# First mixer: the rows of a block inversion in sixteen pieces between the heads' queries and values

## The chip, the core and the metric

One core of one Trainium2 chip runs the whole program. The metric is the time of one execution on the device in microseconds. The engines named below are PE (TensorE: matmuls and transposes through the identity), DVE (VectorE), ACT (ScalarE), POOL (GpSimd) and SP (SyncE, which here only issues DMAs).

## What is computed

The program is a decoder trunk of two layers on 512 tokens of width 1024, in float32. Each layer is a SwiGLU block, a mixer, and another SwiGLU block. The change touches the mixer of the first layer, which runs two groups of heads on one normalised input and projects their concatenation:

```python
def even_mixer(u, w_in, conv_w, a_log, dt_bias, head_norm_w, w_out):
    '''Parallel head groups: dilated sliding-window attention (A) | gated DeltaNet (B).'''
    proj = (u @ w_in).astype(jnp.float32)
    ...
    o_a = dilated_window_attention(qa, ka, va)          # 8 heads of 64
    qkv_b = jax.nn.silu(causal_dwconv(qkv_b, conv_w))   # 4 heads of 128
    ...
    o_b = gated_delta_rule(l2norm(qb), l2norm(kb), vb, g, beta)
    o_b = rmsnorm(o_b, head_norm_w) * jax.nn.silu(z.reshape(bsz, seq, B_HEADS, B_HEAD_DIM))
    o = jnp.concatenate([o_a..., o_b...], axis=-1)
    return (o @ w_out).astype(u.dtype)

def gated_delta_rule(q, k, v, g, beta):
    ...
    a_mat = jnp.where(strict, jnp.einsum('bnhid,bnhjd->bnhij', k_beta, kc) * decay, 0.0)
    t_mat = a_mat + jnp.eye(B_CHUNK, dtype=a_mat.dtype)
    u = lax.linalg.triangular_solve(t_mat, vc * bc, left_side=True, lower=True, unit_diagonal=True)
    w = lax.linalg.triangular_solve(t_mat, k_beta * jnp.exp(gc)[..., None], ...)
    ...
    def step(state, inp): ...      # over the chunks, one after the other
```

The kernel works with 4 chunks of 128 tokens. The triangular systems are solved by an explicit inverse: the 32x32 blocks on the diagonal are inverted row by row on DVE, and two doubling steps with matmuls make 128x128 inverses of them.

## The kernel before

**The mixer.** `even_mixer` has two streams of work. `gated_delta` computes the DeltaNet heads in this order: `keys(h)` for four heads, `invert32` (the 32x32 inverses, for all heads and chunks at once), `queries(h)`, `values(h)`, the two doubling steps (lines 766 to 777), the products with the inverse (780 to 785) and the recurrence over four chunks (787 to 814). I call the part from line 765 to 814 the solve. `attention` computes the attention heads two by two: projections of q and k (each 24 matmuls of 512 columns), projections of the values va for four heads at a time, and for each head four blocks of scores with their softmax (PE, DVE, ACT, DVE, ACT, PE).

**The order.** Both are Python generators. `attention` yields, after each piece that it has written, a number that stands for the piece's length: 5.2 for q or k, 2.6 for each of four pieces of va, and 0.3, 0.6, 0.9 and 1.2 for the four softmax blocks of a head. `gated_delta` yields how much of the attention is to be written next, and the loop (`need -= next(fill, need)`) writes pieces until that is used up; what a piece goes over is lost. What remains of the attention is written when `gated_delta` has ended. After it come the gates (line 900 on), with four projections Z of 24 matmuls each, and the mixer's output product.

The order of writing is a priority: the framework that compiles the kernel orders each engine's instructions ahead of time, by priority, and where the next one isn't ready in its own plan, it puts a later one in its place. On the chip each engine then runs its list in that fixed order. Tiles of one name take turns in a fixed number of slots: `scr` (`scratch()`, 128x512) has 2, `feat` has 2, the PSUM banks `mm` have 2 and `acc` 4. A tile that is written into a slot waits for the last reader of the one that was there.

**The inversion.** `invert32` stops at two yields. Up to the first it stores A to DRAM and loads it in another layout (`nb`, line 707, in a slot of `U`); the result tile `tb` takes one of the two slots of `feat`. Behind it: one ACT instruction turns the sign (711), and a loop of 31 rows follows. Row i is a product (718) of `n x m` elements on DVE into the scratch tile `pr` and a sum over m of it (719) into row i of `tb`, from which the next row reads. `pr` is taken once (line 710), ahead of the loop, and is held to its end. Then one DMA writes `tb` to DRAM (720) and eight DMAs bring the pieces to their places in `Tm` (723).

**Scratch elsewhere.** `queries(h)` takes three scratch tiles: `th` in `conv_silu` (478 and 479), `sq` (737, read by 740) and `er` (a DMA by SP, line 557, then exp on ACT, 746, and a product on POOL, 747). `values(h)` takes one (`th`) and one slot of `feat`; `Rk` (782, POOL) takes one for each head in the solve.

Of the kernel before, what the change touches and what calls it, by code (L numbers as in the profile page):

```python
# [30 lines left out]
class Trunk:  # L31
# [540 lines left out]
    def even_mixer(self, w_in, conv_w, a_log, dt_bias, head_norm_w, w_out, post_w, next_pre):  # L572
# [8 lines left out]
        with ExitStack() as ctx:  # L581
# [52 lines left out]
            def t4(name, bufs=HB):  # L634
                return gp.tile([128, TT, 128], F32, name=name, bufs=bufs)

            def two(name):
                return gp.tile([128, 2 * TT, 128], F32, name=name, bufs=2)

            def transposed(x):  # L640
                p = blocks(self.ps("acc"))
                for c in range(TT):
                    nc.tensor.transpose(p[:, c, :], x[:, c, :], self.ident)
                return p

            def four(lhs, rhs):
                p = blocks(self.ps("acc"))
                for c in range(TT):
                    nc.tensor.matmul(p[:, c, :], lhs[:, c, :], rhs[:, c, :], start=True, stop=True)  # L649
                return p  # L650

            def feature(j, p, out=None):

                out = t4("feat", 2) if out is None else out
                self.conv_silu(p, taps(j), None, out.rearrange("p c t -> p (c t)"))
                return out

            def project(j):
                p = self.ps("mm")
                self.product(p, self.w_cols(w_in, CONV0 + j * 128))  # L660
                return p
# [31 lines left out]
            def invert32():  # L693


                nb = two("U").rearrange("p a b -> p (a b)").rearrange("p (j i) -> p j i", i=32)
                tb = t4("feat", 2).rearrange("p c t -> p (c t)").rearrange("p (i c) -> p i c", c=16)
                ablk = self.dram.tile([4, HB * TT, 32, 32], F32, name="ablk")
                tblk = self.dram.tile([2, 4, HB * TT, 32, 16], F32, name="tblk")
                for b in range(4):  # L700
                    s = slice(32 * b, 32 * b + 32)
                    nc.sync.dma_start(ablk[b].rearrange("q j i -> j q i"), AT[s, :, s])
                nc.gpsimd.memset(Tm, 0.0)
                nc.gpsimd.memset(tb, 0.0)
                for e in range(2):
                    half = slice(64 * e, 64 * e + 64)
                    nc.sync.dma_start(nb[half], ablk.rearrange("b q j i -> (b q) j i"))
                    nc.gpsimd.memset(tb[half, 16 * e:16 * e + 16, :].rearrange("p a b -> p (a b)")[:, ::17], 1.0)
                yield
                pr = self.scratch()  # L710
                nc.scalar.activation(nb, nb, AF.Copy, scale=-1.0)

                nc.gpsimd.memset(nb.rearrange("p a b -> p (a b)")[:, 16 * 33::33], 1.0)
                for i in range(1, 32):
                    n, m = min(i, 16), i + (i >= 16)
                    q = pr[:, :n * m].rearrange("p (c m) -> p c m", c=n)
                    a = nb[:, :m, i:i + 1].rearrange("p m o -> p o m").to_broadcast([128, n, m])
                    tt(q, a, tb[:, :m, :n].rearrange("p m c -> p c m"), op=OP.mult)
                    nc.vector.tensor_reduce(tb[:, i, :n], q, axis=mybir.AxisListType.X, op=OP.add)
                nc.sync.dma_start(tblk.rearrange("e b q i c -> (e b q) i c"), tb)  # L720
                for e in range(2):
                    for b in range(4):
                        nc.sync.dma_start(Tm[32 * b:32 * b + 32, :, 32 * b + 16 * e:32 * b + 16 * e + 16],
                                          tblk[e, b].rearrange("q i c -> i q c"))
                yield

            def values(h):
                vt = t4("vt")
                tt(vt, transposed(feature(2 * HB + h, project(2 * HB + h))), over(col(kl, h)), op=OP.mult)
                return vt  # L730
# [19 lines left out]
            def gated_delta():  # L750
                heads = range(HB)
                K = []
                for h in heads:
                    K.append(keys(h, first[h]))
                    yield 4
                inv = invert32()
                next(inv)
                Q = []
                for h in heads:
                    Q.append(queries(h, *K[h][1:]))  # L760
                    yield 4
                next(inv)
                vt = [values(h) for h in heads]
                yield 4
                U = [part(x, i) for x in (two("U"), two("U")) for i in range(2)]
                for h in heads:
                    nc.scalar.copy(U[h], transposed(part(Tm, h)))
                for l in range(2):
                    for h in heads:
                        Al = t4("kT")  # L770
                        nc.gpsimd.tensor_tensor(Al, part(AT, h), lmask[:, l:l + 1, :].to_broadcast([128, TT, 128]),
                                                op=OP.mult)
                        X = t4("kT")
                        nc.scalar.copy(X, four(Al, part(Tm, h)))
                        tt(U[h], U[h], four(X, U[h]), op=OP.subtract)
                        if l == 0:
                            nc.scalar.copy(part(Tm, h), transposed(U[h]))
                wT = [part(AT, h) for h in heads]
                for h in heads:
                    k = K[h][0]  # L780
                    Rk = blocks(self.scratch())
                    nc.gpsimd.tensor_tensor(Rk, k, over(col(egc, h)), op=OP.mult)
                    nc.scalar.copy(wT[h], four(Rk, U[h]))
                    tt(vt[h], four(U[h], vt[h]), over(col(beta, h)), op=OP.mult)
                    nc.gpsimd.tensor_tensor(k, k, over(col(edec, h)), op=OP.mult)
                S = None
                for c in range(TT):
                    vn = [vt[h][:, c, :] for h in heads]
                    if c:
                        p = blocks(self.ps("acc"))  # L790
                        for h in heads:
                            nc.tensor.matmul(p[:, h, :], wT[h][:, c, :], S[:, h, :], start=True, stop=True)
                        for h in heads:
                            stt(vn[h], p[:, h, :], nbeta[:, c, h:h + 1], vn[h], op0=OP.mult, op1=OP.add)
                    if c + 1 < TT:
                        p = blocks(self.ps("acc"))
                        for h in heads:
                            nc.tensor.matmul(p[:, h, :], K[h][0][:, c, :], vn[h], start=True, stop=True)
                        Sn = t4("S", 2)
                        if S is None:  # L800
                            nc.scalar.copy(Sn, p)
                        else:
                            for h in heads:
                                stt(Sn[:, h, :], S[:, h, :], egl[:, c, h:h + 1], p[:, h, :], op0=OP.mult, op1=OP.add)
                    o = blocks(self.ps("acc"))
                    for h in heads:
                        if c:
                            nc.tensor.matmul(o[:, h, :], Q[h][:, c, :], S[:, h, :], start=True, stop=False)
                        nc.tensor.matmul(o[:, h, :], K[h][2][:, c, :], vn[h], start=c == 0, stop=True)
                    S = Sn  # L810
                    nc.scalar.copy(ob[:, c, :, :], o)
                    junk = self.scratch()
                    for h in heads:
                        nc.scalar.activation(junk[:, :128], ob[:, c, h, :], AF.Square, accum_out=os_[:, c, h:h + 1])

                flat = lambda x: x.rearrange("p c h -> p (c h)")
                rq = self.rstd(flat(qs), 1, 128.0 ** -0.5)
                for _ in range(2):
                    tt(flat(os_), flat(os_), rq, op=OP.mult)
                r = self.rstd(flat(os_), 128)  # L820
                tt(flat(os_), r, rq, op=OP.mult)
# [79 lines left out]
            for need in gated_delta():  # L901
                while need > 0:
                    need -= next(fill, need)
# [322 lines left out]
```

## Time and profile before

| | us |
|---|---|
| three runs, median | 2157.63 |
| three runs, lowest and highest | 2151.29 and 2346.45 |
| the profiled execution | 2155.2 |
| its span, first to last instruction | 2153.4 |

The page gives busy times and shares of the span for each engine, the chain of work that ended last, and the costliest groups of instructions. Answers of the trace give the same for a stretch of the span, in us from its start. A matmul's record overlaps that of the next one, so PE counts as busy as long as matmuls follow each other closely; what is missing from a full stretch is time in which PE stood. The mixer of the first layer lies between about 365 and 690 us, and the inversion's rows between 493 and 559 us.

### The profile page before, as it was taken

Reading aid. Unit: us, or ns where it says so; the run is one execution under the profiler, and the core shown is the slowest. Engines: PE = TensorE matmul, PEld = TensorE weight load, DVE = VectorE, ACT = ScalarE, POOL = GpSimd, SP = SyncE. Lnnn points to the kernel's source line nnn. Section 1 sums busy time; section 2 is a strip of 40 time slices with the busy share of each in tenths; the row PEclk is TensorE's granted clock in tenths of the full one; section 3 lists DMA queues with packets and bytes.
Section 4 is the critical chain, followed back from the end, with each engine's and each line's share of the span. In section 5 each row is a group of like instructions: output and inputs, shape, how many; then the busy total and the mean of one; then the engine's idle time right before and its main releaser. Section 6 shows DMA issues by size and latency. Waiting matters only on the chain.

```text
span 2153.4 us, 33155 instructions
## 1 busy us (share of the span) xinstructions
PE 2111.5 (98%) x13311; PEld 1871.1 (87%) x13311; DVE 1477.5 (69%) x2329; ACT 1024.9 (48%) x1577; POOL 149.5 (7%) x142
## 2 busy tenths in 40 slices
PE   8999999999999999999999999999999999999998
PEld 7999988887788999988899998887777788999986
DVE  5867656869667676656677765678887846867663
ACT  4444553455564444444344454347565423544541
POOL 0011000111110011000001100000000000011000
PEclk9999999999999999999999999999999999999999
DMA  8587424442423588443557842333433236587421
GB/s 235 138 195 159 135 90 138 108 117 56 108 69 98 149 205 185 118 137 108 146 127 181 186 130 93 98 96 90 116 101 100 84 118 157 138 198 160 122 89 68
DMA packets 284037, 277.06 MB, mean 129 GB/s; under 512 B 18576, under 2 KB 244552, under 8 KB 283884
## 3 DMA queue, kind: packets, MB, share of 16 engines
q1 hardware_dynamic: 243308, 228.81, 35.4%
q0 software_dynamic: 40576, 46.14, 12.9%
q8 instruction: 104, 1.70, 0.3%
q14 instruction: 49, 0.40, 0.1%
HBM read 265.93 MB, written 4.79 MB: 126 GB/s over the span
## 4 chain that ended last, share of the span: by engine, by line
PE 84%; DVE 6%; DMA 4%; ACT 3%; issue 2%; POOL 0%; SPq 0%; DVEq 0%; POOLq 0%; ACTq 0%
PE mm L300 18%; PE acc L300 13%; PE acc L235 9%; PE acc L236 9%; PE acc L237 9%; PE mm L167 4%; PE mm L168 4%; PE mm L169 4%; DMA wraw<-in_ffn_w_up_dram 2%; DMA M<-rows_o 1%; PE acc L649 1%; PE acc L169 1%; PE acc L168 1%; PE acc L167 1%; DVE wlo L81 1%
## 5 line engine op out<-in xcount | busy, mean ns | idle before, releaser
L80 ACT CAST whi<-wraw 128x1024 fp32r<-128x1024 f32 x296 | 310.0, 1048 | 396.1 <-PE acc L237 107.4
L81 DVE TENSOR_TENSOR wlo<-wraw,whi 128x1024 fp32r<-128x1024 f32 x292 | 356.8, 1223 | 148.8 <-ACT whi L80 147.0
L80 ACT CAST whi<-wq 128x1024 fp32r<-128x1024 f32 x144 | 151.1, 1049 | 244.7 <-issue 77.6
L167 PE MATMUL mm<-uhi,whi 128*128 128x512 f32 (+1 forms) x712 | 264.5, 372 | 2.1 <-DVE feat L476 1.2
L168 PE MATMUL mm<-ulo,whi 128*128 128x512 f32 (+1 forms) x712 | 262.7, 369 | 0.3 <-DVE ulo L81 0.3
L169 PE MATMUL mm<-uhi,wlo 128*128 128x512 f32 (+1 forms) x712 | 262.6, 369 | 0.0
L81 DVE TENSOR_TENSOR wlo<-wq,whi 128x1024 fp32r<-128x1024 f32 x144 | 175.6, 1222 | 97.3 <-ACT whi L80 93.1
L235 PE MATMUL acc<-whi,hs 128*128 128x512 f32 x576 | 227.2, 395 | 0.0
L236 PE MATMUL acc<-wlo,hs 128*128 128x512 f32 x576 | 227.2, 394 | 0.0
L300 PE MATMUL mm<-uhi,whi 128*128 128x256 f32 x576 | 164.4, 285 | 4.4 <-DVE q L388 4.4
L380 POOL DMA_DIRECT2D wq<-in_ffn_w_up_dram x72 | 92.7, 1291 | 1073.9 <-DMA wq<-in_ffn_w_gate_dram 243.3
L300 PE MATMUL mm<-uhi,wlo 128*128 128x256 f32 x576 | 163.7, 284 | 0.0
L300 PE MATMUL mm<-ulo,whi 128*128 128x256 f32 x576 | 163.6, 284 | 0.0
L300 PE MATMUL acc<-uhi,whi 128*128 128x256 f32 x576 | 162.8, 283 | 0.0
L300 PE MATMUL acc<-uhi,wlo 128*128 128x256 f32 x576 | 162.8, 283 | 0.0
L300 PE MATMUL acc<-ulo,whi 128*128 128x256 f32 x576 | 162.8, 283 | 0.0
L167 PEld LDWEIGHTS mm<-uhi,whi 128*128 128x128 f32 x712 | 134.3, 189 | 27.8 <-issue 4.2
L168 PEld LDWEIGHTS mm<-ulo,whi 128*128 128x128 f32 x712 | 134.7, 189 | 23.6 <-issue 4.1
L169 PEld LDWEIGHTS mm<-uhi,wlo 128*128 128x128 f32 x712 | 134.7, 189 | 22.8 <-issue 3.4
L237 PE MATMUL acc<-whi,hs 128*128 128x512 f32 x384 | 151.5, 395 | 0.0
L236 PEld LDWEIGHTS acc<-wlo,hs 128*128 128x128 f32 x576 | 108.4, 188 | 25.2
L235 PEld LDWEIGHTS acc<-whi,hs 128*128 128x128 f32 x576 | 108.5, 188 | 25.2
(393 smaller groups left out, 5280.0 us busy)
## 6 DMA issues: line engine op xcount, KB each, us to landing
wraw<-in_ffn_w_down_dram SPq DMA_DIRECT2D x88, 512.0 KB, 3.5
wq<-in_ffn_w_gate_dram SPq DMA_DIRECT2D x72, 512.0 KB, 5.6
wq<-in_ffn_w_up_dram POOLq DMA_DIRECT2D x72, 512.0 KB, 8.0
wraw<-in_ffn_w_gate_dram SPq DMA_DIRECT2D x52, 512.0 KB, 5.6
wraw<-in_ffn_w_up_dram SPq DMA_DIRECT2D x52, 512.0 KB, 6.4
wraw<-in_odd_w_in_dram SPq DMA_DIRECT2D x40, 512.0 KB, 4.0
wq<-in_ffn_w_up_dram SPq DMA_DIRECT2D x36, 512.0 KB, 3.8
wraw<-in_even_w_in_dram SPq DMA_DIRECT2D x28, 512.0 KB, 4.6
```

Of the source, the lines that this page charges most:

```text
L80: nc.scalar.copy(hi, src)
L81: (nc.gpsimd if on_pool else nc.vector).tensor_tensor(lo, src, hi.bitcast(F32), op=OP.subtract)
L167: nc.tensor.matmul(p, whi[:, k, :], hi, start=k == 0, stop=False)
L168: nc.tensor.matmul(p, whi[:, k, :], lo, start=False, stop=False)
L169: nc.tensor.matmul(p, wlo[:, k, :], hi, start=False, stop=k == KD - 1)
L235: nc.tensor.matmul(p, ahi, hi, start=k == 0, stop=False)
L236: nc.tensor.matmul(p, ahi, lo, start=False, stop=False)
L237: nc.tensor.matmul(p, alo, hi, start=False, stop=k == nk - 1)
L300: self.nc.tensor.matmul(p[:, f * 256:(f + 1) * 256].rearrange("p (t c) -> p t c", c=128), l, r, start=new and f == k == i == 0, stop=f == ...
L380: nc.gpsimd.dma_start(raw, src, accum_op=OP.add)
L649: nc.tensor.matmul(p[:, c, :], lhs[:, c, :], rhs[:, c, :], start=True, stop=True)
```

## The change

The rows are divided into sixteen pieces. `invert32` yields after a row when the rows so far have reached the next sixteenth of a sum in which row i counts 300 + 2·min(i,16)·i; the pieces are rows 1 to 5, 6 to 9, 10 to 12, 13 to 14, 15 to 16, 17 to 18, 19, 20 to 21, 22 to 23, 24, 25, 26 to 27, 28, 29, 30 and 31. The last one ends with the DMAs of lines 720 and 723. Three pieces are written after each head's queries and one after each head's values. `pr` is now taken anew for every row.

The attention's share is changed too: 5 instead of 4 after each head's keys, 1.7 after each of the three pieces behind a head's queries (4 before, once a head), and 2 after each head's values (4 before, once for all). By the lengths that `attention` yields, and with what pieces go over, 48.4 of it stood ahead of the solve before (q and k of the first two pairs, va and the softmax of heads 0 to 3, and q of the third pair), and 70.0 now: also k of the third pair, va of heads 4 to 7 and the softmax of heads 4 and 5. Behind it remain q and k of the last pair and the softmax of heads 6 and 7. Nothing is computed differently, and the number of instructions of each kind is the same.

```diff
                 yield
-                pr = self.scratch()
                 nc.scalar.activation(nb, nb, AF.Copy, scale=-1.0)
 
                 nc.gpsimd.memset(nb.rearrange("p a b -> p (a b)")[:, 16 * 33::33], 1.0)
+
+                steps, size = 0, lambda i: 300 + 2 * min(i, 16) * i
+                total = sum(size(i) for i in range(1, 32))
                 for i in range(1, 32):
+                    pr = self.scratch()
                     n, m = min(i, 16), i + (i >= 16)
                     q = pr[:, :n * m].rearrange("p (c m) -> p c m", c=n)
                     a = nb[:, :m, i:i + 1].rearrange("p m o -> p o m").to_broadcast([128, n, m])
                     tt(q, a, tb[:, :m, :n].rearrange("p m c -> p c m"), op=OP.mult)
                     nc.vector.tensor_reduce(tb[:, i, :n], q, axis=mybir.AxisListType.X, op=OP.add)
+                    if i < 31 and sum(size(r) for r in range(1, i + 1)) * 16 >= total * (steps + 1):
+                        steps += 1
+                        yield
...
                 for h in heads:
                     K.append(keys(h, first[h]))
-                    yield 4
+                    yield 5
                 inv = invert32()
                 next(inv)
                 Q = []
                 for h in heads:
                     Q.append(queries(h, *K[h][1:]))
-                    yield 4
-                next(inv)
-                vt = [values(h) for h in heads]
-                yield 4
+                    for _ in range(3):
+                        next(inv, None)
+                        yield 1.7
+                vt = []
+                for h in heads:
+                    vt.append(values(h))
+                    next(inv, None)
+                    yield 2
+                for _ in inv:
+                    pass
```

## Rows read from the trace of the kernel before

**Rows 1.** The page: span, and busy time, share and instructions of two engines.

```profile
span 2153.4 us, 33155 instructions
PE 2111.5 (98%) x13311; PEld 1871.1 (87%) x13311; DVE 1477.5 (69%) x2329; ACT 1024.9 (48%) x1577; POOL 149.5 (7%) x142
```

**Rows 2.** The page: chain of work that ended last, shares by engine.

```profile
PE 84%; DVE 6%; DMA 4%; ACT 3%; issue 2%; POOL 0%; SPq 0%; DVEq 0%; POOLq 0%; ACTq 0%
```

**Rows 3.** Windows (stretch, length, busy PE PEld DVE ACT POOL, PEclk, DMA share, GB/s).

```profile
444.00:493.00 49.00, 49.00 (x250) 39.07 (x249) 30.57 (x67) 29.65 (x63) 7.84 (x6) 1.00 0.45 115
493.00:559.00 66.00, 60.24 (x317) 48.17 (x317) 63.06 (x142) 29.58 (x57) 6.77 (x5) 0.97 0.27 75
559.00:626.00 67.00, 66.34 (x463) 57.68 (x464) 33.17 (x92) 41.63 (x108) 15.71 (x13) 1.00 0.24 61
```

**Rows 4.** Waits of PE from 493 to 560 us: total, times, longest.

```profile
PE tr L847 <- ACT P L840: 2.3, 1, 2.3
PE tr L847 <- DVE h L858: 2.0, 1, 2.0
PE mm L167 <- DVE feat L476: 1.2, 2, 0.7
```

**Rows 5.** Window, columns as in Rows 3, around and behind the wait of 2.0 us.

```profile
507.00:515.00 8.00, 6.19 (x21) 4.42 (x22) 6.79 (x23) 2.97 (x8) 0.17 (x1) 0.79 0.25 66
```

**Rows 6.** Groups on DVE, 493 to 559 us: busy us, mean ns, idle before.

```profile
L718 DVE TENSOR_TENSOR scr<-U,feat 128x1 f32<-128x1 f32 (+30 forms) x31 | 18.7, 603 | 0.2
L719 DVE TENSOR_REDUCE feat<-scr 128x1 f32<-128x1 f32 (+30 forms) x31 | 12.4, 400 | 0.2
```

**Rows 7.** Timeline of DVE: first row, the last values, the last row.

```profile
493.42 0.16 DVE L718 TENSOR_TENSOR scr<-U,feat 128x1 f32<-128x1 f32 x1
...
536.53 0.67 DVE L729 TENSOR_TENSOR vt<-acc,kl 128x512 f32<-128x512 f32 x1
...
557.83 0.69 DVE L719 TENSOR_REDUCE feat<-scr 128x16 f32<-128x512 f32 x1
```

**Rows 8.** Timeline of SP behind the last row: start us, us.

```profile
558.55 0.34 SPq L720 DMA_DIRECT2D tblk<-feat  x1
...
560.58 4.32 SPq L723 DMA_DIRECT2D h<-tblk  x8
```

**Rows 9.** Scratch slots on POOL: start us, us, idle before and its releaser.

```profile
455.92 1.29 POOL L747 TENSOR_TENSOR qf<-qf,scr 128x512 f32<-128x512 f32 x1 [1.24 <-ACT scr L746]
534.73 1.05 POOL L782 TENSOR_TENSOR scr<-k,egc 128x512 f32<-128x512 f32 x1 [27.56 <-DVE feat L479]
558.60 1.96 POOL L782 TENSOR_TENSOR scr<-k,egc 128x512 f32<-128x512 f32 x1 [21.09 <-DVE feat L719]
```

**Rows 10.** Timeline of SP and ACT: two scratch tiles `er` and the sign.

```profile
448.98 0.35 SPq L557 DMA_DIRECT2D scr<-rows_e  x1
457.03 1.06 ACT L711 ACTIVATE U<-U 128x1024 f32<-128x1024 f32 x1
480.86 0.63 ACT L746 ACTIVATE scr<-scr 128x512 f32<-128x512 f32 x1 [2.01 <-DMA scr<-rows_e]
```

**Rows 11.** Pieces of the chain, and two matmuls of 512 columns in a row.

```profile
552.65 0.39 PE L168 MATMUL mm<-ulo,whi 128*128 128x512 f32 x1
552.88 0.39 PE L169 MATMUL mm<-uhi,wlo 128*128 128x512 f32 x1
601.86 8.30 PE acc L649 x72
```

**Rows 12.** Groups on PE, 559 to 626 us: solve's largest and last, one of softmax.

```profile
L649 PE MATMUL acc<-U,kT 128*128 128x128 f32 x64 | 9.1, 285 | 0.6 <-ACT kT L774 0.6
...
L169 PE MATMUL mm<-uhi,wlo 128*128 128x512 f32 x11 | 4.6, 419 | 0.0
L831 PE MATMUL tr<-k,q 128*128 128x512 f32 (+3 forms) x12 | 4.6, 380 | 0.0
...
L643 PE MATMUL acc<-ident,h 128*128 128x128 f32 x16 | 1.9, 273 | 0.0
```

## The prediction

> **What bounds the kernel now.** I read the page first. PE is busy for 98% of the span, DVE for 69% [rows 1], and in the chain of work that ended last PE holds 84% [rows 2]. So the end is set by PE: a change in order alone can win only time in which PE stands or runs at a lower clock, and it can lose by making PE stand elsewhere. The number of instructions is the same, so the question is how much PE stands around the inversion's rows.
>
> The next view is the busy time by stretch [rows 3]. From 444 to 493 us, ahead of the rows, PE is busy for all 49.00 us, with DVE at 30.57 (62%). From 493 to 559 us, while the rows run, DVE is busy for 63.06 of 66.00 us (96%), and PE for 60.24: it stands 5.8 us. From 559 to 626 us, in the solve, DVE falls to 33.17 of 67 (50%), and PE stands 0.7 us. The reader should see a stage in which DVE is the bound for 66 us inside a program that is bound by PE.
>
> Third, the waits of PE in the stretch [rows 4]: 2.3 us for a softmax result on ACT, 2.0 us for the line that ends a head on DVE (L858), 1.2 us for a convolution on DVE. With one of 0.2 us that is not shown they make 5.7, the 5.8 us of the windows. Fourth, the clock: from 507 to 515 us the granted clock is 0.79 in the mean [rows 5], so some of the stretch behind the 2.0 us wait was at 1.2 GHz instead of 2.4; 0.21 x 8.00 = 1.7 us. All that the rows seem to cost PE is then 5.7 + 1.7 = 7.4 us, 0.34% of the span.
>
> Last, the timeline. The rows run from 493.42 to 558.5 us [rows 7], 65 us, although their 62 instructions are 18.7 + 12.4 = 31.1 us of work [rows 6]. In the gaps DVE does the values and the attention. The last values end at 537.2 us [rows 7]; the remaining 21 us belong to rows 23 to 31 and the attention's splits.
>
> **The change part by part.** *Work.* Nothing is added or removed: 31 products, 31 sums, one sign change (1.06 us on ACT, and already run at 457.03 us, far ahead of the rows [rows 10]), the same nine DMAs. Cost 0.
>
> *Rows earlier.* The rows' input is ready at 458 us [rows 10], so pieces behind the first queries can run from about there instead of from 493. DVE's work from 444 to 559 us is 30.57 + 63.06 = 93.6 us [rows 3], 81% of 115 us if it is spread evenly. What does PE stand at 81%? The bounds come from the two stretches: 0 as at 62%; or, on a straight line from 62% (no loss) to 96% (5.8 of 66 us, 8.7%), 8.7% x 19/34 = 4.9%, which is 5.6 us in 115 us, so that nothing is won but the clock. Waits for a queue grow faster than its load, and the two long ones [rows 4] are links of a softmax chain that had row instructions of up to 1 us between its own. I take the middle of the two ends, 2.8 us, and no stretch at 1.2 GHz, which here came behind a wait of 2.0 us. Gain 7.4 - 2.8 = 4.6 us; bounds 1.8 and 7.4.
>
> *Scratch.* `pr` held one of the two slots of `scr` for the whole loop. The slots go round in the order of writing: `Rk` on POOL, whose inputs were ready long before, got the first only when the last values' `th` had been read (534.73, waiting for L479) and the second when the last row was done (558.60, waiting for L719) [rows 9]. Now the other users have two slots, a small gain that I leave at 0; but each row asks for one anew, and of the two rows behind a head's queries the second has to wait until that head's `er` has been read by POOL: from the issue at 448.98 [rows 10] to 455.92 + 1.29 = 457.2 [rows 9] is 8.2 us. A planned wait costs nothing, since other DVE work stands ahead of the row. A landing later than planned stops DVE, and with it the splits, convolutions and softmax blocks queued behind the row, for which PE waits. ACT shows that size: it stood 2.01 us for the landing of `er`, for one head of four [rows 10]. Bounds: 0, and 4 x 2.0 = 8.0 us if all four are late and PE has no matmuls queued. I take one such wait with half of it reaching PE: 1.0 us.
>
> The Trainium skill (Perfetto Trace Analysis, Optimization Strategy) says that the same gap coming back on an engine that should be saturated can mean too little SBUF for the next tile. By it, two slots shared by 31 more takers would argue for the upper bound; no row here shows such a gap repeating.
>
> *More attention ahead of the solve.* 70.0 against 48.4 in the attention's own lengths. In the trace the attention ran ahead of what was written: by 559 us the last head of the first two pairs was done and the third pair under way, since gaps were filled. So the added writing moves mainly the softmax of heads 4 and 5. What is behind the solve's start must cover its latency: the solve has ten groups of short matmuls from 559 to 626 us, x64 down to x16, together 328 [rows 12]; at 8.30 / 72 = 0.115 us [rows 11] they are 37.8 us, so 66.3 - 37.8 = 28.5 us was cover. Of that six groups of matmuls of 512 columns (q, k, Z; x11 down to x8, together 56 [rows 12], at 552.88 - 552.65 = 0.23 us each [rows 11]) were 12.9, and 12 softmax blocks [rows 12] the other 15.6, 1.3 each. After the change q and k of the last pair (48 x 0.23 = 11.0), the softmax of two heads (8 x 1.3 = 10.4) and the two Z projections for which `mm` has banks (11.0) are 32.4 us. That is 3.9 us more than is needed: cost 0, and up to 28.5 - 21.4 = 7.1 us if the Z projections can't come forward.
>
> *The end of the inversion.* The last row now stands behind all values and behind head 4's softmax instead of 21 us after the values. Head 4 brings 4 x 1.3 = 5.2 us of PE's time forward, and the saved standing takes 4 to 7 off; the DMA of line 720 should start within 4 us of 558.55 [rows 8]. On SP the nine DMAs keep their place ahead of the output product's weights: line 723's eight issues take 4.32 us as before [rows 8]. Cost 0. Behind the solve PE is the bound again, so the time that PE saves comes off the end.
>
> *Sum.* -4.6 + 1.0 = -3.6 us. Against the profiled execution (2155.2 us: span 2153.4 and 1.8 around it) 2151.6. That execution lies between the lowest run, 2151.29, and the median, 2157.63; I don't shift for that.
>
> **The rivals.**
>
> *Full interleaving.* The Trainium skill (same page and section) says that where the most contended engine changes from stage to stage, interleaving the stages may help. As a mechanism of this kernel: over 444 to 559 us neither engine is full (PE 109.2, DVE 93.6 of 115 us [rows 3]), so PE stands for nothing and the lower clock goes: 2155.2 - 7.4 = 2147.8 us. For it speaks the stretch at 62%, with no wait at all; against it, 81% is nearer to the full stretch. Chance 0.12.
>
> *It doesn't spread.* A row is ready only when the one ahead of it is done and its slot is free, and the engine's order is fixed by a plan, not by the chip. If the plan still lets most rows gather around the values, the stage stays bound by DVE: 2155.2 us, chance 0.12. The rows of one stretch would again hold DVE above 95%.
>
> *Scratch stops DVE (slower).* Place: the second row behind each head's queries, ahead of which POOL must have read `er`. Price: four landings 2.0 us late, all reaching PE, 8.0 us; with the 4.6 gained 2155.2 + 3.4 = 2158.6 us. It decides from 4.6 / 4 = 1.2 us per head. For it: the 2.01 us wait on ACT [rows 10]. Against it: three of four heads showed no such wait, and PE had matmuls queued. Chance 0.15.
>
> *The solve runs short of cover.* If the Z projections stay behind, PE stands 7.1 us in the solve: 2151.6 + 7.1 = 2158.7 us. Against it: Z ran inside the solve before. Chance 0.08.
>
> **How the numbers follow.** The forecast, 2151.6 us, has 0.50; its own range is 2147.8 to 2155.2, from the bounds of its terms. With the rivals (0.12, 0.12, 0.15, 0.08) that is 0.97; 0.03 is left for an order that upsets more than one stage. All named cases lie between 2147.8 and 2158.7 us. The kernel's run of 2151.29 and its median lie 3.9 below and 2.4 above the profiled one, so the measured time may lie that far off: 2144 to 2161. Within 2% (43 us, about what a measurement of this kernel can tell from no change) lie all named cases: 0.97. The 0.03 goes to slower with 0.02 and to faster with 0.01, since no more than 7.4 us is there to be won.
>
> **What the profile of the changed kernel would show.** Right: the rows' first instruction near 455 us and their last near 555, DVE near 80% from 450 to 555 us without a stretch above 95%, PE waiting under 3 us in that time, and no mean clock of 0.79 there. Scratch: idle time of DVE ahead of L718 that ends with POOL's L747 or the landing of `er`. Short of cover: waits of PE between the DMA of line 723 and the end of the recurrence (line 814). Bunched: the rows still within some 65 us. Wrong in kind: a time below 2144, or a shift of waits in a later stage, which I have priced at nothing, for its instructions are written in the same order.

## The result and the profile after

The changed kernel takes 2164.06 us (median of 15 runs, 2159.27 to 2168.9); the kernel before, run beside it as often, 2151.29 us. The ratio is 1.0054, 95% interval 1.0043 to 1.0066; it goes by the fast runs alone and leaves out one run of before at 2346.45 us. The change costs some 12 us. The forecast was 2151.6 us, a gain of 3.6 us on the profiled execution of before, and the time lies above its range (2144 to 2161).

The profiled execution of the changed kernel took 2159.6 us, with a span of 2157.8. Its page gives the same work as [rows 1], with 98% on PE, and nearly the same shares of the chain of work that ended last as [rows 2].

```profile
span 2157.8 us, 33158 instructions
PE 2114.4 (98%) x13311; PEld 1871.7 (87%) x13311; DVE 1481.2 (69%) x2329; ACT 1024.8 (47%) x1577; POOL 149.5 (7%) x142
...
PE 85%; DVE 6%; DMA 3%; ACT 3%; issue 2%; POOL 0%; SPq 0%; DVEq 0%; ACTq 0%; POOLq 0%
```

The two spans differ by 4.4 us only: the profiled execution of after is 4.5 us below its median, and that of before is 3.9 us above its own. Before lost time far ahead of the mixer: near 103 us, in the first feed-forward layer, PE stood 2.2 us and was then at half clock for some 3.3. The stretch in question shows the loss better. Its ends are the last product of the keys (L690 on DVE) and the first matmul of the next layer's weights (L300 on PE). The timelines give, before:

```profile
435.53 1.13 DVE L690 SCALAR_TENSOR_TENSOR AT<-acc,beta,ET 128x128 f32<-128x128 f32 x4
...
740.73 0.28 PE L300 MATMUL mm<-uhi,whi 128*128 128x256 f32 x1
```

and after:

```profile
431.99 1.12 DVE L690 SCALAR_TENSOR_TENSOR AT<-acc,beta,ET 128x128 f32<-128x128 f32 x4
...
746.85 0.28 PE L300 MATMUL mm<-uhi,whi 128*128 128x256 f32 x1
```

That is 305.2 us before and 314.9 after: 9.7 us lost inside the mixer. Where, the windows of after say (columns as in [rows 3], with the same first two stretches):

```profile
444.00:493.00 49.00, 46.42 (x232) 35.56 (x232) 41.26 (x107) 29.71 (x63) 7.78 (x6) 1.00 0.33 89
493.00:559.00 66.00, 58.09 (x295) 46.73 (x293) 46.39 (x93) 27.81 (x55) 4.42 (x2) 0.92 0.30 79
...
568.00:636.00 68.00, 67.06 (x463) 57.81 (x462) 32.67 (x85) 37.98 (x97) 18.10 (x15) 1.00 0.21 53
```

```profile
500.00:512.00 12.00, 9.08 (x34) 6.79 (x35) 7.53 (x18) 6.72 (x15) 0.00 (x0) 0.72 0.42 111
512.00:522.00 10.00, 7.14 (x47) 6.24 (x46) 9.98 (x17) 2.35 (x5) 4.42 (x2) 1.00 0.43 104
```

The reader should see three things. DVE's work is spread, as the change intends: 41.26 of 49 us and 46.39 of 66 us, against 30.57 and 63.06 in [rows 3], and in all 87.7 of 115 us, 76%. Yet PE stands more: 115 - 46.42 - 58.09 = 10.5 us, against 5.8 before. And the granted clock of the second stretch is 0.92 against 0.97: 66 x 0.08 = 5.3 us of clock, against 2.0. Together that is 8.1 us more than before, in the very stretch where 4.6 were to be won. The solve behind it (568 to 636 us, 0.94 us of standing) is as full as before.

The waits of PE from 440 to 570 us (total, times, longest) are other ones than in [rows 4]:

```profile
PE tr L865 <- DVE PTl L81: 2.8, 1, 2.8
PE tr L859 <- ACT P L852: 2.8, 2, 2.4
PE tr L843 <- DVE amax L848: 1.7, 2, 1.4
PE mm L167 <- DVE va L81: 1.5, 1, 1.5
```

The rows start at 450.51 us and end at 569.9 us (DVE's timeline), the four values end at 570.9, and the DMA behind the last row (now L726) starts 11.4 us later than the 558.55 of [rows 8]:

```profile
450.51 0.66 DVE L721 TENSOR_TENSOR scr<-U,feat 128x1 f32<-128x1 f32 x1
...
569.23 0.69 DVE L722 TENSOR_REDUCE feat<-scr 128x16 f32<-128x512 f32 x1
...
570.16 0.69 DVE L735 TENSOR_TENSOR vt<-acc,kl 128x512 f32<-128x512 f32 x1
```

```profile
569.94 0.34 SPq L726 DMA_DIRECT2D tblk<-feat  x1
```

The groups on DVE (busy us, mean ns, idle before) show a thing that no forecast named. The same 31 products take 22.1 us instead of the 18.7 of [rows 6], while the sums take the same 12.4:

```profile
L721 DVE TENSOR_TENSOR scr<-U,feat 128x1 f32<-128x1 f32 (+30 forms) x31 | 22.1, 712 | 1.0 <-POOL qf L753 0.5
L722 DVE TENSOR_REDUCE feat<-scr 128x1 f32<-128x1 f32 (+30 forms) x31 | 12.4, 400 | 0.4
```

### The profile page after: what moved, and what is told of

Same layout as the page of the kernel before. It is cut to its first block, busy times and chain, and to the rows that moved or that the text cites. A ratio compares the mean times of both kernels' runs of the same rounds, so it can differ in the third digit from the quotient of the medians.

```text
span 2157.8 us, 33158 instructions
## 1 busy us (share of the span) xinstructions
PE 2114.4 (98%) x13311; PEld 1871.7 (87%) x13311; DVE 1481.2 (69%) x2329; ACT 1024.8 (47%) x1577; POOL 149.5 (7%) x142
## 4 chain that ended last, share of the span: by engine, by line
PE 85%; DVE 6%; DMA 3%; ACT 3%; issue 2%; POOL 0%; SPq 0%; DVEq 0%; ACTq 0%; POOLq 0%
PE mm L300 18%; PE acc L300 14%; PE acc L235 9%; PE acc L237 9%; PE acc L236 9%; PE mm L167 5%; PE mm L168 5%; PE mm L169 4%; DMA wraw<-in_ffn_w_up_dram 1%; PE acc L649 1%; DMA M<-rows_o 1%; DVE wlo L81 1%; PE acc L169 1%; PE acc L168 1%; PE acc L167 1%
## 5 line engine op out<-in xcount | busy, mean ns | idle before, releaser
L81 DVE TENSOR_TENSOR wlo<-wraw,whi 128x1024 fp32r<-128x1024 f32 x292 | 357.5, 1225 | 153.0 <-ACT whi L80 151.1
L167 PE MATMUL mm<-uhi,whi 128*128 128x512 f32 (+1 forms) x712 | 265.4, 374 | 2.9 <-DVE va L81 1.5
L81 DVE TENSOR_TENSOR wlo<-wq,whi 128x1024 fp32r<-128x1024 f32 x144 | 175.5, 1221 | 97.5 <-ACT whi L80 97.0
L300 PE MATMUL mm<-uhi,whi 128*128 128x256 f32 x576 | 163.5, 284 | 1.6 <-DVE q L388 1.6
L300 PE MATMUL mm<-uhi,wlo 128*128 128x256 f32 x576 | 163.0, 283 | 0.0
L300 PE MATMUL mm<-ulo,whi 128*128 128x256 f32 x576 | 163.0, 283 | 0.0
L300 PE MATMUL acc<-uhi,whi 128*128 128x256 f32 x576 | 162.8, 283 | 0.0
L300 PE MATMUL acc<-uhi,wlo 128*128 128x256 f32 x576 | 162.8, 283 | 0.0
L300 PE MATMUL acc<-ulo,whi 128*128 128x256 f32 x576 | 162.8, 283 | 0.0
L167 PEld LDWEIGHTS mm<-uhi,whi 128*128 128x128 f32 x712 | 134.9, 190 | 29.1 <-issue 4.2
L237 PE MATMUL acc<-whi,hs 128*128 128x512 f32 x384 | 151.5, 395 | 0.0
```

Source lines behind the costliest of these rows:

```text
L81: (nc.gpsimd if on_pool else nc.vector).tensor_tensor(lo, src, hi.bitcast(F32), op=OP.subtract)
L167: nc.tensor.matmul(p, whi[:, k, :], hi, start=k == 0, stop=False)
L237: nc.tensor.matmul(p, alo, hi, start=False, stop=k == nk - 1)
L300: self.nc.tensor.matmul(p[:, f * 256:(f + 1) * 256].rearrange("p (t c) -> p t c", c=128), l, r, start=new and f == k == i == 0, stop=f == ...
```

## DVE instructions that stand still under GpSimd

A group's mean hides which product grew. The timeline gives it. In the mixer `self.share` lets GpSimd take every fifth of the weights' splits (line 94, `wlo`, L81). Of after, POOL first, then what DVE and PE did at the time:

```profile
458.85 2.38 POOL L81 TENSOR_TENSOR wlo<-wraw,whi 128x1024 fp32r<-128x1024 f32 x1 [5.47 <-DVE feat L722]
```

```profile
458.23 0.34 DVE L721 TENSOR_TENSOR scr<-U,feat 128x100 f32<-128x100 f32 x1
...
458.89 0.68 DVE L870 TENSOR_TENSOR h<-tr,P 64x512 f32<-64x512 f32 x1
459.61 1.84 DVE L721 TENSOR_TENSOR scr<-U,feat 128x121 f32<-128x121 f32 x1
461.37 0.41 DVE L848 CUSTOM_DVE_ANT_0 P<-tr,abias 128x256 f32<-128x256 f32 x1
```

```profile
461.84 0.44 PE L843 MATMUL tr<-k,q 128*128 128x384 f32 x1 [1.42 <-DVE amax L848]
```

A product of 121 elements takes 1.84 us, where the one of 100 elements took 0.34. It ends at 461.45 us, 0.2 us after POOL's split (458.85 + 2.38 = 461.23). Behind it on DVE stands the maximum of a softmax block, and PE waits 1.42 us for that. The second place is larger:

```profile
515.62 3.13 POOL L81 TENSOR_TENSOR wlo<-wraw,whi 128x1024 fp32r<-128x1024 f32 x1 [1.56 <-ACT whi L80]
```

```profile
515.38 0.17 DVE L115 TENSOR_TENSOR rs_t<-rs_y 128x16 f32<-128x16 f32 x1
515.57 0.99 DVE L721 TENSOR_TENSOR scr<-U,feat 128x432 f32<-128x432 f32 x1
516.47 2.32 DVE L116 TENSOR_TENSOR rs_t<-rs_t,rs_x 128x16 f32<-128x16 f32 x1
...
519.90 0.67 DVE L81 TENSOR_TENSOR PTl<-tr,PTh 128x512 fp32r<-128x512 f32 x1
```

```profile
520.63 0.50 PE L865 MATMUL tr<-PTl,va 128*128 128x512 f32 x1 [2.84 <-DVE PTl L81]
```

An instruction of 16 elements, 0.17 us for its neighbour L115, takes 2.32 us and ends with POOL's split (515.62 + 3.13 = 518.75). The split itself took 3.13 us instead of 2.38, since DVE's L721 was ahead of it. So each holds up the other, and PE waits 2.84 us at the end of the chain. The waits at the two places are 4.3 of the 10.5 us for which PE stands.

The kernel before had the same thing in it. Its wait of 2.0 us in [rows 4], with the low clock of [rows 5] behind it, follows this place:

```profile
504.79 2.38 POOL L81 TENSOR_TENSOR wlo<-wraw,whi 128x1024 fp32r<-128x1024 f32 x1 [7.47 <-ACT whi L80]
```

```profile
504.99 2.21 DVE L119 TENSOR_TENSOR rs_y<-rs_t,rs_y 128x16 f32<-128x16 f32 x1
```

The Trainium skill (SBUF — State Buffer, SBUF: two separate sides) states that DVE and GpSimd share a pair of ports as an exclusive lock: a DVE instruction with two inputs in SBUF and a GpSimd instruction that reads SBUF wait for each other, whoever starts first. The trace agrees: L119 stood 2.21 us under a split of 2.38, while L870, one of whose two inputs (`tr`) is in PSUM, ran in 0.68 us while another was under way (458.89). I had not weighed it, because [rows 1] give POOL 7% of the span.

## The experiments

All times are against runs of the kernel before on the same chip (medians 2149.65 to 2151.29 us). Three explanations stood against each other for the 12 us: the *order* (the new shares put softmax chains where PE has little else to do), the *scratch slots* (the rows and the other users of `scr` wait for each other), and the *port* (rows and their neighbours stand under GpSimd). A fourth question is what the rows cost at all.

**Which part of the change costs: the pieces or the shares.** Two kernels with one part each. The pieces with the shares of before:

```
K:      yield 5                  ->  yield 4
Q:      3 x (next(inv), 1.7)     ->  3 x next(inv), then yield 4
V:      yield 2 behind each      ->  yield 4 behind all four
```

> The rows in sixteen pieces at their new places, with the attention's shares of before (4 after each head's keys, 4 after the three pieces behind a head's queries, 4 after all values), so that the attention pieces written at each place are those of before. Theory A (row instructions on DVE between the links of the softmax chains make PE wait): still slower than before, 1.004 to 1.006, and PE's waits for softmax results between 445 and 520 us stay. Theory B (more attention written ahead of the values pushes the values and the solve back): 0.998 to 1.001, and the last values end before 545 us.

And the rows in one piece as before, with the shares of after (5; three times 1.7; 2):

> The rows in one piece at their old place, ahead of all values, with one scratch tile held through the loop, but with the attention's new shares (5; 1.7 three times; 2). Theory A: as before, 0.999 to 1.002. Theory B: 1.004 to 1.006, and the values end 15 us or more after their place in the kernel before.

Measured: 2164.33 us, 1.0059 [1.0046, 1.0072], for the pieces alone, and 2162.32 us, 1.0052 [1.0040, 1.0063], for the shares alone. Each part by itself costs as much as both together (1.0054). So the costs don't add, and neither part "has" the loss. The first has the time of theory A and the values of theory B (they end at 543.7 us); the second is as theory B has it, with the values' end at 574.6. In the first the solve ends early, at about 612 us, and the attention is left alone behind it until 660; from 605 to 665 us PE stands 6.1 us:

```profile
605.00:665.00 60.00, 53.87 (x255) 41.46 (x255) 38.47 (x93) 35.34 (x79) 0.00 (x0) 0.97 0.42 132
```

In the second PE waits 8.8 us for convolutions of the values (L167 <- DVE feat L476), which stand between rows on DVE.

**What the rows are worth.** Both kernels with the 62 row instructions left out, and with them the scratch tile `pr` that they use:

```
-    tt(q, a, tb[:, :m, :n].rearrange("p m c -> p c m"), op=OP.mult)
-    nc.vector.tensor_reduce(tb[:, i, :n], q, axis=mybir.AxisListType.X, op=OP.add)
```

> The kernel before without the 62 row instructions, so the inverse of each 32x32 block is left as the unit matrix; everything else runs. It measures what the rows cost PE in their old place. By the waits and the clock of the profile before, 7.4 us: 0.9966 of before. If the waits are the softmax chain's own, they stay and the ratio is 0.999 to 1.000.

> The changed kernel without the 62 row instructions (the same part left out). Theory A: the same time as the kernel before without its rows, within 0.1%. Theory B: 8 to 12 us above that one, 0.4 to 0.5% more.

Measured: 2152.57 us, 1.0010 [1.0001, 1.0018], and 2148.85 us, 0.9995 [0.9986, 1.0004]. Taking 31 us of DVE's work out of its fullest stretch, and freeing a scratch slot, makes the kernel before no faster, which neither of its two forecasts had. The changed kernel without rows is 0.15% below it, so theory B is out and theory A nearly right. The windows of the first show why, with the end of the attention beside them:

```profile
493.00:576.00 83.00, 82.77 (x567) 73.14 (x568) 42.95 (x91) 42.99 (x100) 20.93 (x17) 1.00 0.23 64
576.00:650.00 74.00, 67.18 (x306) 50.83 (x305) 46.44 (x119) 44.54 (x96) 0.00 (x0) 0.93 0.34 107
```

The 7.4 us that the rows seemed to cost are gone: from 493 to 576 us PE stands 0.23 us, at full clock. But the solve then ends at 576 us instead of 629, and the rest of the attention has only itself to fill its gaps: from 576 to 650 us PE stands 6.8 us and the clock is 0.93, another 5.2 us. The same stretch of the kernel before has 0.24 us of standing:

```profile
576.00:626.00 50.00, 49.96 (x372) 44.49 (x372) 24.24 (x68) 29.58 (x81) 10.58 (x9) 1.00 0.15 40
626.00:650.00 24.00, 23.80 (x115) 18.64 (x114) 19.33 (x48) 15.82 (x32) 0.00 (x0) 1.00 0.37 117
```

So the slow rows were not a pure loss. They kept the solve late enough to serve as cover for the softmax chains at the end. What the rows cost in their stage is given back in the next. With the rows the changed kernel is 0.59% slower than without them (some 13 us); the kernel before is 0.1% faster with than without.

**The scratch slots.** The kernel before with only this moved into the loop, so that every row asks for a slot:

```
-    pr = self.scratch()
     for i in range(1, 32):
+        pr = self.scratch()
```

> The kernel before with one edit of the change: each row takes a scratch tile of its own; rows, values and shares stand as before. If the slots matter (a row waits for another user, or the values' convolutions no longer wait for the one free slot): 1.002 to 1.005 or 0.997 to 0.999. If they don't: 0.9995 to 1.001.

Measured: 2186.77 us, 1.0163 [1.0147, 1.0179], the largest loss of all and far above what was expected. The longest wait of PE from 480 to 560 us, a window, and the timelines of ACT and DVE:

```profile
PE acc L643 <- DVE feat L479: 17.7, 1, 17.7
```

```profile
516.00:538.00 22.00, 4.02 (x12) 2.90 (x12) 20.00 (x28) 1.48 (x3) 0.00 (x0) 0.50 0.08 24
```

```profile
535.18 0.63 ACT L478 ACTIVATE scr<-feat 128x512 f32<-128x512 f32 x1 [15.34 <-DVE feat L719]
```

```profile
535.18 1.04 DVE L718 TENSOR_TENSOR scr<-U,feat 128x512 f32<-128x512 f32 x1
536.13 0.69 DVE L479 SCALAR_TENSOR_TENSOR feat<-scr,feat 128x512 f32<-128x512 f32 x1
536.74 0.69 DVE L719 TENSOR_REDUCE feat<-scr 128x16 f32<-128x512 f32 x1
```

The slots of `scr` go out in the order in which the program is written. All 31 rows are written ahead of the values, so the values' `th` (line 477, written by L478) gets its slot behind the last of them: ACT waits 15.34 us for a sum over a row (L719), and L479 runs at 536.13, right behind the last product. PE stands 17.7 us for it, at half clock. So asking for a slot in every row is a real cost, but not by the mechanism of the prediction: DVE did not stop for a landing of `er` here, the values stopped for the rows. The changed kernel avoids this by writing the last rows between the values: there each of the four `th` waits for its own input (L478 <- DVE feat L476), 1.4 us at most, and none for a slot. Its values end at 570.9 us, where they used to end at 537.2 [rows 7], but the slots are not what delays them: with the new shares, one piece and one scratch tile they end at 574.6 us, and with the sixteen pieces and the shares of before at 543.7.

**The port.** With the splits of the mixer kept on DVE (`self.share = True` becomes `False`; the same work, and nothing of it on GpSimd), in both kernels:

> The kernel before with every weight's split on DVE (self.share stays False), so that POOL does none of them. In the profile before, the split on POOL at 504.8 us (2.38 us) lies over a DVE instruction of 16 elements that took 2.21 us instead of 0.17, and PE waits 2.0 us behind it and then runs at 1.2 GHz for a while. Theory C (a POOL instruction that reads SBUF holds up a DVE instruction with two SBUF inputs): 3 to 4 us less, 0.998 to 0.9985. Rival: the splits that move to DVE (1.22 us each) cost as much there: 0.9995 to 1.002.

> The changed kernel with every weight's split on DVE. Its profile has two splits on POOL in the stretch of the rows, over a row product of 1.84 us (others of that size 0.36) and an instruction of 2.32 us (others 0.17); PE's waits of 1.6 and 3.0 us follow them. Theory C: 5 to 7 us less than the changed kernel, 1.002 to 1.003 of before. If the loss is the order of softmax, projections and rows alone: 1.005 as the changed kernel.

Measured: 2145.65 us, 0.9981 [0.9967, 0.9996], and 2152.0 us, 1.0008 [0.9996, 1.0020]. Giving DVE more to do makes both faster, the changed kernel by 0.46% (10 us) and the kernel before by 0.19% (4 us). In the kernel before L119 takes 0.18 us where it took 2.21.

But the gain of the kernel before isn't there. From the last matmul of the feed-forward layer ahead (L237 on PE) to the last L690 it takes 64.1 us with the shared splits and 58.8 without; the changed kernel takes 63.8 and 58.9. So both win 5 us ahead of the rows, among the keys, where a GpSimd split held up an instruction of four elements and PE waited 2.39 us. In the kernel before:

```profile
421.78 3.11 POOL L81 TENSOR_TENSOR wlo<-wraw,whi 128x1024 fp32r<-128x1024 f32 x1 [24.70 <-ACT whi L80]
```

```profile
422.56 2.34 DVE L116 TENSOR_TENSOR rs_t<-rs_t,rs_x 128x4 f32<-128x4 f32 x1
```

```profile
425.56 0.39 PE L198 MATMUL mm<-whi,uhi 128*128 128x256 f32 x1 [2.39 <-DVE k L81]
```

From L690 to L300 the kernel before takes 304.8 us instead of 305.2: without the block at L119 other waits appear (1.5 us for `k`, 1.0 for `h`). That its ratio is the one of theory C is therefore luck, for theory C looked for the gain at L119. The changed kernel takes 309.0 us there instead of 314.9; with the 5 us among the keys it wins more than theory C had summed from the two places beside the rows. (The waits of 1.6 and 3.0 us that the expectation names are the 1.42 and 2.84 above.) The port's part in the change is what this stretch gives, 5.9 - 0.4 = 5.5 us, for the gain among the keys is in both kernels.

Then the queries' product on GpSimd moved as well, so that no tensor_tensor of GpSimd runs beside the rows:

```
-    nc.gpsimd.tensor_tensor(flat, flat, er, op=OP.mult)
+    tt(flat, flat, er, op=OP.mult)
```

> The kernel after with the splits of the mixer and also the product of the queries (L753) off GpSimd, so that no GpSimd tensor_tensor runs beside the row pieces. Against the kernel with the splits alone moved (1.0008, 2152.0). Port theory: the piece products that stood 1.7 us under L753 fall back to 0.36 us and up to 3 us are gained, 2149. If VectorE's own load is what counts there (four products of some 0.6 us more on VectorE), no gain: 2152 to 2154.

Measured: 2149.54 us, 0.9992 [0.9979, 1.0005]. The products fall back to the 18.7 us of [rows 6]:

```profile
L721 DVE TENSOR_TENSOR scr<-U,feat 128x1 f32<-128x1 f32 (+30 forms) x31 | 18.7, 604 | 0.4
```

This step's own gain (0.9992 against 1.0008) isn't certain, for the intervals overlap and the mixer's stretch differs by 0.3 us in the two profiles. What PE still waits for in that kernel from 440 to 570 us are links of the softmax (1.7 us for `P`) and of the attention's queries and values (2.8 us for `q`, 1.4 for `va`).

And the pieces with the shares of before, on DVE throughout:

> The kernel after with the shares of before (4, 4, 4) and with the splits of the mixer kept off GpSimd. With GpSimd sharing the splits it ran at 1.0059, and without the sharing the kernel before runs at 0.9981. Port theory (the sixteen pieces lose because their products and their neighbours stand under GpSimd's splits): the pieces then cost nothing, about 2146, 0.998. Cover theory (the pieces bring the solve's end ahead of the attention's, which is left alone at the end, 17.0 us of excess there against 6.1): the loss of the last phase stays, about 2154 to 2157, 1.002 to 1.004.

Measured: 2148.82 us, 0.9994 [0.9981, 1.0006], against 1.0059 with the shared splits. That lies between the two expectations. Moving the splits gains this kernel 14 us, of which 12.1 lie between L690 and L300 (320.3 and 308.2 us), and some of the loss at the end stays: from 605 to 650 us PE stands 2.3 us, where the kernel before is full:

```profile
605.00:650.00 45.00, 42.67 (x201) 32.66 (x200) 34.20 (x83) 28.59 (x57) 0.00 (x0) 1.00 0.48 150
```

**The values in one go.** The four values with the last pieces between them, but no attention between; all of it behind:

```
     for h in heads:
         vt.append(values(h))
         next(inv, None)
-        yield 2
     for _ in inv:
         pass
+    yield 11.5
```

> The changed kernel, but the four values with the last four pieces are written one after the other, and the attention's 11.5 that stood between and behind them comes after all four. Theory D (the new shares take the values' projections, which need little of DVE, away from where they cover the softmax of the second pair): the values end some 10 us earlier, but the softmax of heads 2 and 3 still stands ahead of them, so the loss stays, 1.004 to 1.006. Theory E (the loss comes from the solve starting late): 1.000 to 1.002.

Measured: 2156.56 us, 1.0030 [1.0017, 1.0043], 0.0024 better than the changed kernel and between the two theories. The values end 9.5 us earlier, as theory D says; the wait for `va` (1.5 us) is gone from the stretch, and the others are the same. With the splits on DVE too:

> The kernel after with the four values in one go, the last four pieces behind them, and the splits of the mixer off GpSimd. Values in one go gave 1.0030, the splits alone 1.0008, against 1.0054 of the kernel after. If the two causes are separate and add up, 1.0054 - 0.0024 - 0.0046 = 0.9984, about 2146.5, no better than the kernel before with the same splits (0.9981). If the values took their time from the splits (one cause twice), about 1.0008, 2151.

Measured: 2148.51 us, 0.9988 [0.9975, 1.0001]. That is near the sum of the two (0.9984), and no better than the kernel before with the same splits, which at 2145.65 us remains the fastest of all the kernels run and the only one whose interval lies below 1.

**Read together.** With GpSimd sharing the splits, six orders of the whole work lie between 1.0000 and 1.0163, five of them without the scratch kernel between 1.0000 and 1.0059. With the splits on DVE four of these orders lie between 0.9981 and 1.0008. So about half of the change's loss hangs on GpSimd: between the two kernels the difference is 0.54% with the shared splits and 0.27% (1.0008 against 0.9981) with the splits on DVE. With POOL quiet beside the rows as well it is 0.11% (0.9992), too small to tell from none, but the kernel before was not run with that last edit. In the profiles the stretch from L690 to L300 keeps 309.0 - 304.8 = 4.2 us of the 9.7, and 3.8 with POOL quiet (735.16 - 426.52 = 308.6 against 731.23 - 426.44 = 304.8). The rest goes with the shares, and the kernels without rows show them at work. In the changed one PE stands 5.4 us from 493 to 559 us, at a clock of 0.92, though no row runs, where the kernel before without rows stands 0.23 at full clock (its window above):

```profile
493.00:559.00 66.00, 60.57 (x313) 49.77 (x312) 38.30 (x83) 30.72 (x60) 6.65 (x4) 0.92 0.29 84
```

```profile
PE mm L167 <- DVE q L81: 1.9, 1, 1.9
PE tr L855 <- ACT P L848: 1.9, 1, 1.9
PE mm L167 <- DVE va L81: 1.5, 1, 1.5
```

None of these waits has a GpSimd split over it (those run at 460.1 and 510.2 us). The one for `P` has a weight's split of 1.22 us on DVE (494.23 us) ahead of the softmax's reciprocal. With its rows the changed kernel stands 10.5 us in the same stretch and loses 5.3 of clock. So 5.4 and 5.3 of that are there without any row, and what the rows and the port add is 5.1 us, about the 4.3 of the two places above. Without rows the changed kernel is no slower in the end, because from 576 to 650 us it stands 0.4 us at full clock, where the kernel before without rows loses 12.0. With the rows in, the kernel before stands only 0.24 us there, and nothing is to be had. That the shares are the whole rest isn't shown: with the shares of before and the splits on DVE the pieces take 308.2 us from L690 to L300, 3.4 more than the kernel before, though none of the new shares is in them. Moving the splits also moves the planned order of DVE. The port's part is therefore shown directly only at the places in the timelines above, and the rest of its size is by difference.

## Why the prediction was wrong, step by step

**What is at stake.** I took the 5.7 us of waits [rows 4] and 1.7 us of clock [rows 5] as the price of the rows and the most that could be won. Wrong: without rows the kernel before takes 2152.57 us. The waits go, as the sum said, and 12.0 us come up behind the solve. The sum ended at 559 us; the solve's date was not in it. I had said that a shift of waits into a later stage was priced at nothing, and that is one of the three steps that failed; the other two are *Rows earlier* and *More attention ahead of the solve*.

**Rows earlier.** This is the term with the wrong sign. I made PE's standing a function of DVE's load: 2.8 us at 81%, at most 5.6. The load came out as forecast, even lower (76%), and PE stood 10.5 us with 5.3 us of clock. In place of the gain of 4.6 us stands a loss of 15.8 - 7.7 = 8.1 us, most of the 9.7 us by which the mixer's stretch grew. (2155.2 + 8.1 = 2163.3 us lies close to the 2164.06 measured by luck: the first number is of a profiled execution 3.9 us above its median.) A load says how much time is free, not which instruction stands ahead of which. Of the four long waits of after, two have a blocked DVE instruction at their head (1.4 and 2.8 us). The longest of those for ACT, 2.4 us, is a softmax chain whose reciprocal stood on DVE behind a weight's split of 1.22 us (500.46 us); no row was in between. I had also put the 2.0 us wait of [rows 4] down to row instructions between its links; most of it was the 2.21 us of L119, with three row instructions (507.12 to 508.04 us) behind it.

**The clock.** I assumed no stretch at 1.2 GHz. The granted clock was 0.72 from 500 to 512 us, and it fell when PE had stood 2.41 us for a softmax, as it had fallen behind a wait of 2.0 us before. It was 0.83 from 540 to 550 us, behind the wait of 1.5 us for `va`:

```profile
502.35 0.69 PE L859 MATMUL tr<-ident,P 128*128 128x128 f32 x2 [2.41 <-ACT P L852]
```

The step is wrong because the waits did not go. And the length of a wait alone doesn't tell: behind the 2.84 us wait the clock was 1.00 (522 to 530 us), and in the kernel before it was 1.00 from 530 to 559 us, with the 2.3 us wait of [rows 4] in that stretch.

**Scratch.** Forecast 1.0 us by rows that wait for `er`. DVE waited for POOL's `qf` (L753) 0.5 us in all, so the rival "scratch stops DVE" did not happen as told, though its total (2158.6) had the right sign. Where the slots can cost is elsewhere: in one piece the values' `th` queues behind the rows, for 35 us (1.63%). In the sixteen pieces no `th` of the values waits for a slot, and the trace shows no cost of the slots beyond the 0.5 us. I had these rows before me [rows 9] and drew from them only that the other users gain.

**More attention ahead of the solve.** Cost 0 behind the solve's start holds: from 568 to 636 us PE stands 0.94 us. The rival "short of cover" did not happen. But the other end of the step was never priced: what is written earlier stands with its chains and its weights' splits among the queries. That is where the cost 0 was wrong: without any row the changed kernel stands 5.4 us there and loses 5.3 of clock, and the shares alone, with the rows in one piece, cost 0.52%.

**The end of the inversion.** Forecast within 4 us of 558.55, measured 569.94, 11.4 us later: the last row is tied to the last value, and the values are late by the new shares (574.6 us even with the rows in one piece) and by PE's standing.

**The rivals and the signs named.** No stretch of DVE above 95%: wrong, 9.98 of 10 us from 512 to 522. Rows from 455 to 555: 450.5 to 569.9. PE waiting under 3 us: 10.5. "It doesn't spread" is out: the rows took 119 us instead of 65. "Full interleaving" rested on a rule of the Trainium skill (Perfetto Trace Analysis, Optimization Strategy), that interleaving stages may help where the contended engine changes. Here the load did even out, and the kernel lost 0.54%. The range was too narrow because only the scratch rival let the order add standing inside the stretch, and that by another mechanism. Nor is 2% what a measurement of this kernel can just tell from no change: the interval of the ratio is 0.23% wide.

## What to carry to other kernels

Before pricing a change of order, look in the timeline for instructions that take much longer than their twins, and at what GpSimd runs at that time: an engine at 7% can set the waits of one at 98%. Before counting the standing of an engine as a gain, ask what the late work covers later: leave the work out, and see whether the whole becomes faster. And where tiles of a pool go round in the order of writing, a loop that asks for one each time joins the queue of every other user.

## What the runs showed of the hardware

A tensor_tensor of 128x16 on DVE, 0.17 us by itself, took 2.21 and 2.32 us beside a GpSimd tensor_tensor of 128x1024, and a row product of 128x121 took 1.84 us instead of 0.36 (its time with POOL quiet). GpSimd's split took 2.38 us when it came first and 3.13 us when a DVE product of 0.99 us was ahead of it, so the holding up goes both ways. Moving such splits from GpSimd to the busier DVE, where one took 1.22 us, made two kernels faster, by 4 and by 10 us. Not every block costs as much: by difference the gain among the keys was some 5 us, that beside the rows in pieces 5.9, and that around the block at L119 0.4.
